# A hybrid attention and recurrence layer: the first block's keys beside the meta keys, squares by halves, and the last scalings shared with ScalarE

## The chip, the core and the metric

The kernel runs on one core of a Trainium2 chip. The metric is the device time of one execution in microseconds (us). PE is TensorE, the matmul engine; DVE is VectorE, ACT ScalarE, POOL GpSimd; SP is the engine whose queue issues most of the loads. "PEld" in a view is PE's loading of stationary operands.

## What is computed

One decoder layer over 1024 tokens of width 1024, with 16 learned meta tokens put ahead of them (1040 rows in all):

```
u = rmsnorm(h, g_pre_mix);  q, k, v, xr, yr = split(u @ w_in)
attn = sliding_window_attention_with_sinks(q, k, v, sinks)   # window 128
rec  = gelu(yr) * rg_lru(conv4(xr))                          # gated recurrence
h = h + rmsnorm(concat(attn, rec) @ w_out, g_post_mix)
u = rmsnorm(h, g_pre_ffn)
h = h + rmsnorm(square(relu(u @ w_ff1)) @ w_ff2, g_post_ffn) # d_ff = 4096
return h[16:]
```

Attention has 8 query heads of 64 and 2 key heads. Queries are taken in blocks of 128. A block sees the 128 keys before it and its own 128; for the first block of real tokens the keys before it are 112 places of padding, which are masked, and the 16 meta tokens. RMSNorm multiplies a row by (mean of squares + 1e-6) to the power -1/2.

## The kernel before, in words

Everything is in float32. A matmul of full precision is made of three: each operand is split into a high part, rounded to the format fp32r, and a low part, the rest; the product is high x high + high x low + low x high (`mm3`, lines 125 to 127; `part`, line 253, does one of the three at a time). The high part is cast on ACT (line 96 in `split`, 309 in `high_w`), the low part is a subtraction on DVE (lines 99 and 313).

The work has these stages in time.

1. **Rows and projections** (about 0 to 58 us). Rows of x come in eight blocks of 128, the meta rows ahead of the first. `norm_rows` (from line 222) squares a block on ACT with the row sum as by-product (line 225), forms rstd on POOL in two steps (lines 164 and 170: add eps, power -1/2) and scales the rows on DVE (line 231). PE transposes them against an identity (line 322); ACT and DVE evict high and low parts, times the norm's gain (lines 117 and 118). For the first 272 columns (meta rows and two blocks) the order on ACT and on DVE is written out by hand: `chained(0, ...)` strings ACT's instructions, `chained(1, ...)` DVE's. ACT's string is: high part of the key weights, the eight evictions, high part of the v weights, of the q weights, the squares of row blocks 3 and 4, the evictions of keys and v, the high part of the x weights. The squares of later row blocks are not in that string.
2. **The keys.** `sink_k` (lines 390 and 394) writes the keys' high and low parts, each head in its half of the partitions. The first projected piece holds 16 meta columns and 256 real ones. The meta keys go to `km`, a constant tile of four parts (head, high or low) of 128 columns, of which the last 16 hold keys and the rest zeros; the real ones go to `khh` (high) and `kl`. A DMA on POOL's queue copies the other half of the partitions (line 489).
3. **Attention** (about 58 to 187 us), in eight steps: four query pairs j times two halves of four blocks. `scores` makes, for each of two heads, a PSUM bank for two blocks at a time: q's block is the stationary operand, keys the moving one, 256 columns high (line 581) and 256 low (line 585). For block 0 that is done in four matmuls of 128 columns: the padded meta keys from `km`, then the first block from `khh` and `kl`. ACT copies scores (599), DVE picks between the two key blocks (600), takes the minimum (607), ACT the exponential (82), DVE scales (616); `attend` transposes on PE (630), splits, masks on POOL (635) and multiplies with v (646). Projections of later queries, of the recurrence's inputs and of its gates (`next_fill`) run between as filling work of lower priority.
4. **The recurrence**, the output projection and the first feed-forward product (to about 560 us).
5. **The second feed-forward product**, from there to the end, as seven products in place of eight (`PLAN`), each of eight steps. In the last product the last three steps are kept back and done output block by output block (`finish_late`), so that blocks 0, 1 and 2 can be finished while PE works on the next; block 3's columns are done in two pieces of 256. Finishing is: add the last product into the sum (`combine`, line 951), square it with the row sum (line 1284 on ACT, or line 1334 on DVE for block 3), root on ACT (line 82), reciprocal on DVE (189), scale by rstd and gain, and write. Blocks 0 to 2 are scaled by DVE in one instruction of 1024 columns (line 1327) and added into `out` by an accumulating DMA on POOL's queue (line 1331). For block 3 the multiplication by the gain is done ahead of the root (line 951) and two instructions scale and add the residual (line 1345). `finish_half` (line 1306) prepares the halves that are complete earlier.

Where no order is written out, a planner simulates the program with estimated costs and emits each engine's instructions in the order that comes out, by priority (place in the program) among what is ready. `behind(name, ins)` holds an instruction behind another in that order without a semaphore. On the chip each engine works through its list in order.

Tiles come from slots with tags: "ws" has 4, "b" 17, "c" 8, "d" 4, "e" 2, "raw" 2; a new tile of a tag waits until the oldest one's readers are done. PSUM has eight banks, two of each tag "acc", "s", "pt" and "o".

At the very start PE multiplies zeros (`load`, line 284), 7 times 512 and 6 times 256 columns; their result is not read. The zeros were those of `km`, cast by DVE (line 274) from a cleared tile.

## Time and profile before

| what | us |
|---|---|
| time before, median of 3 runs | 959.34 (959.26 to 960.56) |
| the profiled execution | 958.7 |
| its span, first to last instruction | 956.9 |
| PE busy in the span | 944.2 |
| DVE, ACT, POOL busy | 658.8, 501.9, 127.5 |

All views below come from that one profiled execution. Their times count from the start of the span. A timeline row gives start, duration, engine, line of the kernel, operation, tiles (written <- read), shape, and in brackets the idle time of the engine ahead of it with what ended that. The row of a matmul includes the filling of the array, so rows that follow each other on PE overlap; from start to start is what one costs. Where a row says x13, thirteen instructions are merged.

### The profile page before, as it was taken

How to read it: one execution, taken by the hardware profiler on the slowest of the kernel's cores; microseconds unless marked ns; L12 is line 12 of the kernel's file. 1: busy time of each engine (PE TensorE's matmuls, PEld its weight loads, DVE VectorE, ACT ScalarE, POOL GpSimd, SP SyncE). 2: the span in 40 equal slices, each digit the busy share in tenths (PEclk: the TensorE clock that was granted, in tenths of full speed). 3: DMA queues.
4: the chain of work that ended last, by engine and by line, in shares of the span. 5: the costliest groups of instructions: out<-in, count | busy, mean ns of one | idle time of the engine just before them, and what ended most of it. 6: DMA issues, size and time to landing. Idle time of an engine off the chain costs nothing.

```text
span 956.9 us, 12402 instructions
## 1 busy us (share of the span) xinstructions
PE 944.2 (99%) x4731; PEld 789.3 (82%) x4731; DVE 658.8 (69%) x841; ACT 501.9 (52%) x845; POOL 127.5 (13%) x186
## 2 busy tenths in 40 slices
PE   8999999999999999999999999999999999999996
PEld 7999999877888877888888888888888788888885
DVE  6567987879855776665644465476576776769884
ACT  7536666568645554434555575663533343445441
POOL 4102655410021100000000000001111100001201
PEclk9999999999999999999999999999999999999999
DMA  8221101104226466585532354324767765637934
GB/s 268 57 66 23 46 23 46 45 23 122 83 110 192 133 204 214 182 270 164 176 108 90 110 185 124 110 89 132 176 176 176 209 208 179 196 132 205 237 65 88
DMA packets 88183, 130.14 MB, mean 136 GB/s; under 512 B 13718, under 2 KB 52646, under 8 KB 88124
## 3 DMA queue, kind: packets, MB, share of 16 engines
q1 hardware_dynamic: 79532, 106.54, 34.0%
q0 software_dynamic: 8160, 21.51, 10.7%
q10 hardware_dynamic: 432, 1.31, 0.4%
q8 instruction: 37, 0.61, 0.3%
q14 instruction: 22, 0.18, 0.1%
HBM read 109.93 MB, written 18.87 MB: 135 GB/s over the span
## 4 chain that ended last, share of the span: by engine, by line
PE 94%; DVE 3%; ACT 1%; POOL 0%; DMA 0%; issue 0%; SPq 0%; DVEq 0%; POOLq 0%; ACTq 0%
PE ps_acc L125 11%; PE ps_acc L126 11%; PE ps_acc L127 11%; PE ps_pt L125 7%; PE ps_pt L126 6%; PE ps_pt L127 6%; PE ps_s L127 6%; PE ps_s L126 6%; PE ps_s L125 6%; PE ps_o L127 5%; PE ps_o L125 5%; PE ps_o L126 5%; PE ps_o L646 1%; PE ps_acc L253 1%; PE ps_o L925 1%; PE ps_s L581 1%
## 5 line engine op out<-in xcount | busy, mean ns | idle before, releaser
L96 ACT CAST ws<-raw 128x1024 fp32r<-128x1024 f32 (+1 forms) x68 | 69.6, 1024 | 117.8 <-PE ps_o L126 47.6
L99 DVE TENSOR_TENSOR ws<-raw,ws 128x1024 fp32r<-128x1024 f32 (+1 forms) x69 | 82.4, 1194 | 52.7 <-ACT ws L96 52.7
L125 PE MATMUL ps_acc<-a,ws 128*128 128x256 f32 (+2 forms) x256 | 86.1, 336 | 0.0
L126 PE MATMUL ps_acc<-a,ws 128*128 128x256 f32 (+2 forms) x256 | 85.4, 333 | 0.0
L127 PE MATMUL ps_acc<-a,ws 128*128 128x256 f32 (+2 forms) x256 | 85.0, 333 | 0.0
L99 DVE TENSOR_TENSOR b<-b,b 128x1024 fp32r<-128x1024 f32 (+2 forms) x50 | 58.9, 1178 | 26.5 <-PE ps_o L126 17.7
L96 ACT CAST ws<-e 128x1024 fp32r<-128x1024 f32 x41 | 42.9, 1047 | 64.3 <-PE ps_o L126 41.2
L96 ACT CAST b<-b 128x1024 fp32r<-128x1024 f32 (+2 forms) x49 | 50.0, 1020 | 43.8 <-DVE b L951 38.3
L99 DVE TENSOR_TENSOR ws<-e,ws 128x1024 fp32r<-128x1024 f32 x41 | 50.1, 1223 | 24.2 <-ACT ws L96 24.2
L635 POOL TENSOR_SCALAR_AFFINE_SELECT c<-c 128x512 fp32r<-128x512 f32 x64 | 53.7, 857 | 70.5 <-ACT c L96 60.7
L125 PEld LDWEIGHTS ps_acc<-a,ws 128*128 128x128 f32 x256 | 48.3, 189 | 4.8 <-issue 0.2
L126 PEld LDWEIGHTS ps_acc<-a,ws 128*128 128x128 f32 x256 | 48.2, 188 | 4.4 <-issue 0.4
L127 PEld LDWEIGHTS ps_acc<-a,ws 128*128 128x128 f32 x256 | 48.2, 188 | 4.4
L126 PE MATMUL ps_acc<-ws,b 128*128 128x512 f32 (+1 forms) x120 | 46.2, 385 | 0.6 <-DVE ws L99 0.6
L125 PE MATMUL ps_acc<-ws,b 128*128 128x512 f32 (+1 forms) x120 | 46.2, 386 | 0.0
L127 PE MATMUL ps_acc<-ws,b 128*128 128x512 f32 (+1 forms) x120 | 46.2, 385 | 0.0
L125 PE MATMUL ps_pt<-ws,b 128*128 128x512 f32 x112 | 44.4, 396 | 0.0
L126 PE MATMUL ps_pt<-ws,b 128*128 128x512 f32 x112 | 44.1, 394 | 0.0
L127 PE MATMUL ps_pt<-ws,b 128*128 128x512 f32 x112 | 44.0, 393 | 0.0
L125 PE MATMUL ps_s<-ws,b 128*128 128x512 f32 x110 | 43.4, 395 | 0.0
L127 PE MATMUL ps_s<-ws,b 128*128 128x512 f32 x110 | 43.3, 394 | 0.0
L126 PE MATMUL ps_s<-ws,b 128*128 128x512 f32 x110 | 43.3, 393 | 0.0
(399 smaller groups left out, 2658.7 us busy)
## 6 DMA issues: line engine op xcount, KB each, us to landing
raw<-in_w_ff_dram SPq DMA_DIRECT2D x61, 512.0 KB, 4.5
e<-in_w_ff_dram SPq DMA_DIRECT2D x45, 512.0 KB, 3.4
d<-in_w_ff_dram SPq DMA_DIRECT2D x12, 512.0 KB
s_dram<-d POOLq DMA_DIRECT2D x12, 512.0 KB, 4.1
raw<-in_w_in_dram SPq DMA_DIRECT2D x9, 512.0 KB
c<-in_x_dram SPq DMA_DIRECT2D x8, 512.0 KB
d<-in_x_dram SPq DMA_DIRECT2D x8, 512.0 KB, 3.2
out_dram<-raw SPq DMA_DIRECT2D x8, 512.0 KB
```

What stands on the lines that cost most here:

```text
L96: nc.scalar.copy(hi, src)
L99: low = nc.vector.tensor_tensor(lo, src, f32(hi), op=ALU.subtract).ins
L125: nc.tensor.matmul(dst, lh, rh, start=start, stop=False, skip_group_check=True)
L126: nc.tensor.matmul(dst, lh, rl, start=False, stop=False, skip_group_check=True)
L127: last_mm[0] = nc.tensor.matmul(dst, ll, rh, start=False, stop=stop, skip_group_check=True).ins.name
L253: last_mm[0] = nc.tensor.matmul(acc[:, :n], w[k // 2][:, kc, :], u[kc][k % 2][:, t0 : t0 + n], start=k == 0 and kc == 0, stop=k == last an ...
L581: nc.tensor.matmul(dst, q[h][:, c], hi, start=True, stop=False, skip_group_check=True,)
L635: nc.gpsimd.affine_select(out=p_[:, :, s], in_=f32(p_[:, :, 0]), pattern=[[0, 4], [g, P]], compare_op=op, fill=0.0, base=0, channel_multip ...
L646: nc.tensor.matmul(po[:, oc : oc + n], v, p_[:, pc : pc + n], start=first and k == 0, stop=last and k == 1, skip_group_check=True,)
L925: nc.tensor.transpose(pt[:, i, :], xn[:, kc * P : (kc + 1) * P], ident)
```

## The change

Four edits.

1. `km` becomes a tile of four parts of 256 columns: 112 zeros, 16 meta keys, and the 128 keys of the first block, which `sink_k` writes in the same instructions as the meta keys (64 x 144 in place of 64 x 16) and the DMA copies to the other half. They are written to `khh` and `kl` as well, as before. Block 0's scores then take two matmuls of 256 columns in place of four of 128. The tile is no longer a constant; it takes a slot of tag "e", the third one asked for, after the raw weights of q and of x; POOL clears it.
2. The zeros for the first products are a cleared "ws" tile, without the cast. All 13 zero products come first, and after each of the eight groups of transposes of the first 272 columns one more of 128 columns is put behind.
3. `norm_rows` of row blocks 1 and 2 (`fast`): ACT squares one half of the columns, DVE the other, POOL adds the two sums (eps is in DVE's) and takes the power, and DVE scales in two pieces of 512.
4. At the end, for blocks 0 to 2 the squares' by-product goes to PSUM. For block 2 the second half is multiplied by the gain beforehand (in `finish_half`), DVE scales only the first half and ACT the second. For block 3's first 256 columns ACT squares in place of DVE and adds the sum so far with one more small instruction; DVE's products by the gain are held behind its squares.

```diff
+        if fast:
+            ss = [small.tile([P, 1], F32, name=f"hq{i}", tag=f"hq{i}") for i in range(2)]
+            nc.scalar.activation(
+                xn[:, :512], src[:, :512], AF.Square, scale=RMS_SC, accum_out=ss[0]
+            )
+            nc.vector.tensor_tensor_reduce(
+                out=xn[:, 512:], in0=src[:, 512:], in1=src[:, 512:], scale=RMS_SC * RMS_SC,
+                scalar=EPS, op0=ALU.mult, op1=ALU.add, accum_out=ss[1],
+            )
+            rs = small.tile([P, 1], F32, name="rs", tag="rs")
+            nc.gpsimd.tensor_tensor(ss[0], ss[0], ss[1], op=ALU.add)
+            nc.gpsimd.tensor_tensor(rs, ss[0], half_pow, op=ALU.pow)
+            for i in range(2):
+                c = slice(512 * i, 512 * i + 512)
+                nc.vector.tensor_scalar(xn[:, c], src[:, c], rs, None, op0=ALU.mult)
+            return xn
...
-    zero = slot("ws", [P, 512])
-    nc.vector.memset(zero, 0.0)
-    km = const.tile([P, 4, P], F32R, name="km")
+    zeros = slot("ws", [P, 512], F32R)
+    nc.vector.memset(f32(zeros), 0.0)
-    nc.vector.tensor_copy(km.rearrange("p a b -> p (a b)"), zero)
...
-    cold = load(7, 512)
+    load(7, 512)
+    load(6, 256)
...
+            if b == 0:
+                load(1, P, ins.ins.name)
...
-    load(6, 256, cold)
...
     low_w(wq, rq)
+    km = slot("e", [P, 4, 2 * P], F32R)
+    nc.gpsimd.memset(f32(km[:, 0:2, 0 : P - NMETA]), 0.0)
+    nc.gpsimd.memset(f32(km[:, 2:4, :]), 0.0)
...
-            m, mk = slice(0, NMETA), slice(P - NMETA, P)
+            m, mk = slice(0, NMETA + P), slice(P - NMETA, 2 * P)
...
-                        qk(sp_[:, i, 0:P], b, km[:, h, :], km[:, 2 + h, :])
-                        qk(sp_[:, i, P:256], b, khh[h][:, 0:P], kl[h][:, 0:P])
+                        qk(sp_[:, i, :], b, km[:, h, :], km[:, 2 + h, :])
...
+        if j > 1:
             behind(w_low[0], combine(o[:, c], acc[:, c], gffn_b[:, c], ALU.mult))
...
             if j < 3:
+                rs = root_rstd(squares(y[k], acc[:, c], 0), ssq)
+                done_ = COLS[0] if j == 2 else slice(0, D)
                 w_low[0] = nc.vector.scalar_tensor_tensor(
-                    o, acc, root_rstd(squares(o[:, c], acc[:, c], 0), ssq), gffn_b,
+                    o[:, done_], acc[:, done_], rs, gffn_b[:, done_],
                     op0=ALU.mult, op1=ALU.mult,
                 ).ins.name
+                if j == 2:
+                    nc.scalar.activation(o[:, COLS[1]], o[:, COLS[1]], AF.Copy, scale=rs)
...
+            if k == 0:
+                part = squares(y[k], acc[:, c], 0)
+                nc.scalar.activation(part, part, AF.Identity, bias=ssq)
+            else:
+                part = small.tile([P, 1], F32, name="part", tag="part")
+                w_low[0] = nc.vector.tensor_tensor_reduce(
+                    out=o[:, c], in0=acc[:, c], in1=acc[:, c], scale=RMS_SC * RMS_SC,
+                    scalar=ssq, op0=ALU.mult, op1=ALU.add, accum_out=part,
+                ).ins.name
...
-            w_low[0] = combine(o[:, c], acc[:, c], gffn_b[:, c], ALU.mult).name
+            ins = combine(o[:, c], acc[:, c], gffn_b[:, c], ALU.mult)
+            if k == 1:
+                behind(w_low[0], ins)
+            w_low[0] = ins.name
```

More of the change, by code (lines that the diff above doesn't have):

```diff
@@ L220, in hybrid_layer, with norm_rows @@
     RMS_SC = 1.0 / math.sqrt(D)
-    def norm_rows(src, n, link=False):
+    def norm_rows(src, n, link=False, fast=False):
         xn = slot("d", [P, D])
+        if fast:
[14 more added lines that the diff above has]
+            return xn
         ssq = small.tile([P, 1], F32, name="ssq", tag="ssq")
@@ L268, in hybrid_layer @@
         nc.gpsimd.memset(f32(kl[h][HALF[1 - h]]), 0.0)
-    zero = slot("ws", [P, 512])
-    nc.vector.memset(zero, 0.0)
-    km = const.tile([P, 4, P], F32R, name="km")
+    zeros = slot("ws", [P, 512], F32R)
+    nc.vector.memset(f32(zeros), 0.0)
     vm = const.tile([P, 2, P], F32R, name="vm")
-    nc.vector.tensor_copy(km.rearrange("p a b -> p (a b)"), zero)
     flip = [0]
     idle = bank("acc")
-    zeros = km.rearrange("p a b -> p (a b)")
     def load(n, cols, after=None):
@@ L296, in normed @@
         rows += [(xt[2 * b], P), (xt[2 * b + 1], P)]
-        return [(norm_rows(s[:m], m), m) for s, m in rows]
+        return [(norm_rows(s[:m], m, fast=b == 0 and m == P), m) for s, m in rows]
     last = [None, None]
@@ L486, in hybrid_layer @@
     for h in range(2):
-        r, o, m = HALF[h], HALF[1 - h], slice(P - NMETA, P)
+        r, o, m = HALF[h], HALF[1 - h], slice(P - NMETA, 2 * P)
         nc.gpsimd.dma_start(f32(khh[h][o]), f32(khh[h][r]))
@@ L1326, in finish_late @@
             if j < 3:
+                rs = root_rstd(squares(y[k], acc[:, c], 0), ssq)
+                done_ = COLS[0] if j == 2 else slice(0, D)
                 w_low[0] = nc.vector.scalar_tensor_tensor(
-                    o, acc, root_rstd(squares(o[:, c], acc[:, c], 0), ssq), gffn_b,
+                    o[:, done_], acc[:, done_], rs, gffn_b[:, done_],
                     op0=ALU.mult, op1=ALU.mult,
                 ).ins.name
+                if j == 2:
+                    nc.scalar.activation(o[:, COLS[1]], o[:, COLS[1]], AF.Copy, scale=rs)
                 nc.gpsimd.dma_start(out[j * P : (j + 1) * P, :], o, accum_op=ALU.add)
                 continue
-            part = small.tile([P, 1], F32, name=f"part{k}", tag=f"part{k}")
-            nc.vector.tensor_tensor_reduce(
-                out=o[:, c], in0=acc[:, c], in1=acc[:, c], scale=RMS_SC * RMS_SC,
-                scalar=ssq, op0=ALU.mult, op1=ALU.add, accum_out=part,
-            )
+            if k == 0:
[7 more added lines that the diff above has]
+                ).ins.name
             ssq = part
```

## The prediction

> **What bounds the kernel now.** I read the page first: the span, the busy times and the chain that ended last; then the waits of PE, to see where it ever stood still.

> ```profile
> span 956.9 us, 12402 instructions
> PE 944.2 (99%) x4731; PEld 789.3 (82%) x4731; DVE 658.8 (69%) x841; ACT 501.9 (52%) x845; POOL 127.5 (13%) x186
> ...
> PE 94%; DVE 3%; ACT 1%; POOL 0%; DMA 0%; issue 0%; SPq 0%; DVEq 0%; POOLq 0%; ACTq 0%
> ```

> ```profile
> PE ps_acc L284 <- DVE km L274: 2.4, 1, 2.4
> PE ps_acc L125 <- ACT a L1136: 0.7, 1, 0.7
> PE ps_o L322 <- DVE d L231: 0.6, 2, 0.5
> PE ps_acc L126 <- DVE ws L99: 0.6, 1, 0.6
> PE ps_o L646 <- POOL c L635: 0.6, 1, 0.6
> ```

> PE is busy for 944.2 of 956.9 us and carries 94% of the chain. In between it waits 4.9 us in all, half of it before its first instruction; the other idle time is the tail after its last matmul. So microseconds come from three places only: matmul time itself, those waits, and the tail. A microsecond taken from another engine in the middle is worth nothing unless it ends one of the waits.

> The profiled execution took 958.7 us (1.8 us outside its span), 0.6 under the median of the three timed runs, 959.34. I make the sum against 958.7 and carry the difference over to the median.

> **The start.** Columns of the timeline: start, duration, engine, line, tiles, shape, and in brackets the idle time and what ended it.

> ```profile
> 1.09 2.11 POOL L268 MEMSET b<- 64x1024 f32 x2
> ...
> 1.49 0.83 DVE L274 CAST km<-ws 128x512 fp32r<-128x512 f32 x1
> ...
> 2.38 4.61 PE L284 MATMUL ps_acc<-km 128*128 128x512 f32 x13 [2.38 <-DVE km L274]
> ...
> 6.33 1.06 ACT L225 ACTIVATE d<-c 128x1024 f32<-128x1024 f32 x1 [0.51 <-DMA c<-in_x_dram]
> ...
> 8.47 0.75 DVE L231 TENSOR_SCALAR d<-c,rs 128x1024 f32<-128x1024 f32 x1 [0.81 <-POOL rs L170]
> 8.49 1.05 ACT L309 CAST b<-raw 128x1024 fp32r<-128x1024 f32 x1 [1.02 <-DMA raw<-in_w_in_dram]
> ...
> 9.64 0.49 ACT L117 ACTIVATE a<-ps_o,gcol 128x272 fp32r<-128x272 f32 x1
> ...
> 12.83 4.19 PEld L253 LDWEIGHTS ps_acc<-a,b 128*128 128x128 f32 x33 [0.19 <-ACT a L117]
> ...
> 15.71 1.22 DVE L313 TENSOR_TENSOR ws<-e,ws 128x1024 fp32r<-128x1024 f32 x1
> ...
> 18.36 1.06 ACT L225 ACTIVATE d<-c 128x1024 f32<-128x1024 f32 x1 [1.61 <-DMA c<-in_x_dram]
> ...
> 19.41 0.73 ACT L390 CAST b<-ps_acc 64x256 fp32r<-64x256 f32 x2
> 20.16 0.36 ACT L390 CAST km<-ps_acc 64x16 fp32r<-64x16 f32 x2
> ...
> 20.82 1.05 ACT L309 CAST ws<-e 128x1024 fp32r<-128x1024 f32 x1
> ...
> 21.92 2.04 PEld L253 LDWEIGHTS ps_acc<-a,ws 128*128 128x128 f32 x16
> ```

> **Zeros.** The 0.83 us cast of km goes and PE can multiply zeros at about 1.5 instead of 2.38. Those products are thrown away (the six narrower ones already ran ahead, all 13 are in one row), so the 0.9 us less in the first wait is worth nothing by itself. The eight new 128-wide zero products sit where PE is paced by ACT (it still waits for ACT before 12.83): cost 0, and 8 x 0.11 = 0.9 us (the narrow matmul's time, worked out below) if that cover were gone.

> **Squares by halves.** Now the second row block's square takes ACT 1.06 us from 6.33, then POOL, then DVE's scaling until 9.22. Half a row on ACT (0.63 for 128x512, row at the end) saves about 0.4. DVE's half is not in the trace in this form: 256 columns take it 0.48 (L1334, below), so 512 lie between 0.48 and 0.96; I take 0.75, since 256 and 512 columns of an addition take 0.41 and 0.69. POOL's two steps stay two. The scaling in two pieces costs one more fixed part, about 0.1. If DVE has the second block's square queued behind both scalings of the first, 0.85 us, the 0.4 is gone and xn comes some 0.3 late.

> None of it reaches the end. ACT's first eviction (9.64) has to follow the cast of the key weights, which starts at 8.49 when their DMA lands and ends at 9.54: 0.1 us to be had, whatever the squares do. And there is a second gate. ACT's queue holds the square of the fifth row block ahead of the key eviction; that square waits for its DMA until 18.36. From there ACT runs without a pause: square, keys 19.41, meta keys 20.16, v, cast of the x weights 20.82 to 21.87; PE starts on these weights at 21.92. PE arriving 0.1 earlier or 0.3 later at 21.9 finds nearly the same gate. I take 0, bounds 0.2 gained and 0.3 lost.

> **The wider meta tile costs at that gate.** The two casts of 64x16 (0.18 each) become 64x144. Between 64x16 and 64x256 (0.365 each) a column costs 0.8 ns, so 128 more are 0.1 each: **0.2 us lost**, since everything up to the cast of the x weights moves. Bounds: 0, if the planner puts the keys ahead of that square; 0.4 at the price of 64x256. DVE's two subtractions grow alike; behind them waits the low part of the x weights, which PE asks for only after 16 products with the high part, 2.04 us from 21.92. The wider copies by DMA are wanted at 58.7 (row below).

> km now lies in a slot of tag "e", so POOL may clear it only when the q weights in that slot are split (15.71 + 1.22 = 16.93). POOL's clearing: 1.05 us per 1024 columns, 224 + 512 columns, 0.76 us, done at 17.7 if the queue is free; ACT writes km at 20.16. Behind the clearing stand POOL's rstd steps of the next rows, which PE transposes just before 21.92. All hidden, with 2.4 us of slack; beyond that ACT's queue stops at km, with v and the x weights behind it and PE behind these, and each us costs one. The slot's next user is the gates' weights after the last score (153), so no load waits.

> **Scores.** This is the term that counts.

> ```profile
> L581 PE MATMUL ps_s<-km,b x8: 221/222/307, 58.7 to 153.4; 128*128 128x128 f32 x8
> ```

> ```profile
> 73.04 0.22 PE L581 MATMUL ps_s<-km,b 128*128 128x128 f32 x1
> ...
> 74.20 0.39 PE L126 MATMUL ps_acc<-a,ws 128*128 128x512 f32 x1
> ...
> 79.22 0.28 PE L581 MATMUL ps_s<-b,b 128*128 128x256 f32 x1
> ...
> 80.17 0.60 PE L630 MATMUL ps_pt<-ident,c 128*128 128x128 f32 x4
> ```

> A group with the first block is ten matmuls, four of them 128 wide: 74.20 - 73.04 = 1.16 us. A group without it is eight of 256: 80.17 - 79.22 = 0.95, or 0.119 each. So the four narrow ones cost 1.16 - 6 x 0.119 = 0.45, 0.11 each: hardly less than wide ones. Two wide ones in their place save 0.21, in eight groups 1.7 us.

> [...]

> Does PE time count there?

> ```profile
> 20.00:185.00 165.00, 164.91 (x1222) 155.84 (x1220) 128.19 (x242) 99.99 (x294) 63.93 (x94) 1.00 0.17 44
> ```

> ```profile
> 100.00:120.00 20.00, 20.00 (x135) 18.27 (x134) 19.49 (x31) 13.26 (x40) 10.68 (x16) 1.00 0.19 54
> ...
> 900.00:930.00 30.00, 30.00 (x156) 25.49 (x155) 29.53 (x31) 15.53 (x24) 2.42 (x2) 1.00 0.51 123
> ```

> ```profile
> 151.08 0.77 ACT ws L96
> ...
> 185.50 1.25 PE ps_o L646 x9
> ```

> (Windows: length, then busy time of PE, PEld, DVE, ACT, POOL.) The chain stays on PE up to 151, where ACT takes it over from the scores, and comes back at 185.50 after 0.6 us of waiting. Between, PE works but is not what ends last. Seven of the eight groups lie before 151, the last at 153. I count seven: **1.5 us gained**; bounds 0, if other engines hold the stage, and 1.7.

> **The end.**

> ```profile
> 936.85 0.69 DVE L951 TENSOR_TENSOR a<-ps_acc,a 128x512 f32<-128x512 f32 x1 [6.93 <-PE ps_acc L127]
> ...
> 945.69 0.63 ACT L1284 ACTIVATE a<-a 128x512 f32<-128x512 f32 x1 [3.12 <-DVE a L951]
> ...
> 947.44 1.28 DVE L1327 SCALAR_TENSOR_TENSOR a<-a,rs,a 128x1024 f32<-128x1024 f32 x1
> ...
> 948.63 0.48 DVE L1334 CUSTOM_DVE_ANT_0 a<-a,late 128x256 f32<-128x256 f32 x1
> ...
> 948.90 0.28 PE L127 MATMUL ps_acc<-a,b 128*128 128x256 f32 x1
> ...
> 949.15 0.42 DVE L951 TENSOR_TENSOR a<-a,a 128x256 f32<-128x256 f32 x1
> 949.50 0.41 DVE L951 TENSOR_TENSOR a<-ps_acc,a 128x256 f32<-128x256 f32 x1
> ```

> PE's last matmul ends at 949.18, but DVE adds its result only at 949.50, being busy with block 2's scaling (1.28), the square of block 3's first quarter (0.48) and its product (0.42). After: half the scaling, 0.69, to 948.1; the product to 948.5; DVE waits for PE at 949.18. The last addition comes **0.3 us earlier** and with it all that follows. ACT has three instructions more of at most 0.63 each after 947.4: through by 949.3, and its sum is asked for at 949.6. Squares written to PSUM in place of SBUF I count alike; the block's output goes out earlier, which nothing waits for. Bounds 0 and 0.4. The multiplication brought forward (0.69 on DVE, which is 29.53 of 30 busy up to 930) stands behind the split of a later step's weights; the 6.93 us that DVE idles before 936.85 cover it; else it costs 0.7.

> **Sum.** -1.5 - 0.3 + 0.2 = -1.6 us: 957.1 against 958.7, and 957.7 against the median. That is 0.17%, under the 0.2% (1.9 us) that a measurement of this kernel can tell from no change.

> **Rivals.**

> *PE's time is not passed on.* DVE is at 19.49 of 20 us from 100 to 120, and POOL ended a PE wait at 185.5. If the attention chain keeps its pace, PE only waits longer. Then -0.3 + 0.2: **959.2**. Against it: PE's row has 164.91 of 165 us busy up to the wait at 185, and ACT and DVE are released by the scores. [...]

> *The order falls out well.* The order on each engine is planned anew. If the keys get ahead of the waiting square, the 0.2 is not lost and the 0.2 of the start is kept; if the wait at 185.5 closes, 0.6 more: 957.7 - 1.0 = **956.7**. For it: both waits are products of one order. Against: nothing in the change asks for it.

> *PE stays at half speed*, on the slow side.

> ```profile
> L284 PE MATMUL ps_acc<-km x13: 388/628/792, 2.4 to 6.6; 128*128 128x512 f32 x7, 128*128 128x256 f32 x6
> ```

> A 512-wide zero product takes 628 ns, later ones 390: the zeros warm PE up. With them from 1.5 on they end about 0.9 us earlier, with little behind them until the rows come. Should PE fall back, the 33 matmuls from 12.83 (4.19 us, 0.127 each) take twice that; past 1.6 us lost, 13 of them, the change is slower; all 33 give +2.6: **961.9**. Against: the eight zero products are put there. [...]

> **How the numbers follow.** Forecast 50%, its own range 957.1 to 958.9; not passed on 18%; good order 22%; half speed 10%. Faster by over 0.2% (under 957.4): a third of the forecast and nearly all of the good order, 0.39. Slower (over 961.3): most of the last case, 0.07. The rest, 0.54. The range, 956.0 to 960.0, takes in the first three cases with the bounds of their terms (-1.7, -0.4, -0.2 and the closed wait's 0.6 below; no merge gain and 0.4 + 0.3 lost at the start above) and some tenths of scatter, and leaves out half speed.

> **What would show it.** Right: the score groups with km take 0.95; PE's wait at 185.5 grows slightly; the last DVE addition follows PE's last matmul at once; PE starts on the x weights some 0.2 later than 21.92. Wrong: a new wait of PE between 20 and 185, zeros' successors at 0.25 each, or ACT waiting for POOL before km.

## The result and the profile after

| | kernel before | changed kernel |
|---|---|---|
| median, us (22 executions of each) | 961.25 (959.26 to 963.86) | 959.10 (957.11 to 962.38) |
| the profiled execution | 958.7 | 961.16 |
| its span | 956.9 | 959.5 |
| ratio after / before | | 0.9975, interval 0.9967 to 0.9984 |

The change makes the kernel faster by 0.25%, some 2.4 us (0.16 to 0.33%; 2.15 us between the medians). Forecast were 1.6 us, and 957.7 us as the time; 959.1 lies in the range, but 1.4 us over the forecast although the gain was larger: the base had been taken as 959.34, the median of three executions, and over 22 it is 961.25. Moreover, the profiled execution of the changed kernel is 2.5 us *longer* than that of before. One profile of each can't be compared by its length here; both have to be taken apart by place. The changed kernel's page first:

```profile
span 959.5 us, 12392 instructions
PE 947.1 (99%) x4723; PEld 792.0 (83%) x4723; DVE 658.9 (69%) x845; ACT 501.6 (52%) x849; POOL 126.8 (13%) x188
...
PE 88%; DVE 5%; DMA 2%; ACT 2%; POOL 1%; issue 1%; DVEq 0%; SPq 0%; ACTq 0%; POOLq 0%
```

PE is busy for 2.9 us more than before (944.2), though it has eight products fewer: a busy PE need not be a fast one. And 2% of the chain are DMA, which had none. Next PE's waits (engine, line, releaser: us in all, times, longest):

```profile
PE ps_acc L297 <- DVE base_e L537: 1.5, 1, 1.5
PE ps_s L127 <- DVE e L99: 0.7, 1, 0.7
PE ps_o L336 <- DVE d L239: 0.7, 1, 0.7
PE ps_acc L125 <- ACT a L1154: 0.7, 1, 0.7
PE ps_s L336 <- DVE d L248: 0.5, 1, 0.5
PE ps_o L664 <- POOL c L653: 0.3, 1, 0.3
```

Against before: the wait at the end of attention (L646, now L664) fell from 0.6 to 0.3, where the forecast had it grow; the wait of `ps_s L127` for DVE is new. Its place is 365 us. Four places make up nearly all of the 2.5 us: 3.6 - 2.1 + 1.4 - 0.3.

**Attention.** The start of the last transposes of v and of the first gate matmul, in the timelines of before and of after:

```profile
64.74 0.38 PE L554 MATMUL ps_pt<-ident,c 128*128 128x128 f32 x2
...
197.78 0.43 PE L772 MATMUL ps_s<-b,e 64*128 64x348 f32 x1
```

```profile
68.29 0.38 PE L573 MATMUL ps_pt<-ident,c 128*128 128x128 f32 x2
76.61 0.28 PE L600 MATMUL ps_s<-e,b 128*128 128x256 f32 x1
...
77.54 0.39 PE L127 MATMUL ps_acc<-a,ws 128*128 128x512 f32 x1
...
199.26 0.43 PE L790 MATMUL ps_s<-b,e 64*128 64x348 f32 x1
```

133.04 us before, 130.97 after: **2.07 us gained**. A group of scores with the meta keys takes 77.54 - 76.61 = 0.93, where the prediction had named 0.95 as the sign of being right.

**The start.** It gave 3.6 us away in this execution:

```profile
8.49 1.05 ACT L323 CAST b<-raw 128x1024 fp32r<-128x1024 f32 x1 [1.42 <-DMA raw<-in_w_in_dram]
...
14.60 6.04 PEld L270 LDWEIGHTS ps_acc<-a,b 128*128 128x128 f32 x37
...
20.89 0.75 ACT L408 CAST b<-ps_acc 64x256 fp32r<-64x256 f32 x2 [1.59 <-PE ps_acc L270]
21.66 0.57 ACT L408 CAST e<-ps_acc 64x144 fp32r<-64x144 f32 x2
...
22.26 1.06 ACT L242 ACTIVATE d<-c 128x1024 f32<-128x1024 f32 x1
...
23.72 1.05 ACT L323 CAST ws<-e 128x1024 fp32r<-128x1024 f32 x1
...
25.50 1.55 PEld L270 LDWEIGHTS ps_acc<-a,ws 128*128 128x128 f32 x12
```

The key matmuls take 6.04 us for 37, 0.163 each in the mean, where before had 0.127 (4.19 for 33): from start to start 0.23 until 17.6 us and 0.13 after. PE runs at half clock until then: the trace's records of the granted clock begin at 17.6 us here and at 6.8 before (the windows' clock column counts from there only and shows 1.00 for the stretch ahead; the weight loads' durations tell the truth, 330 ns until 17.1 us and 188 from 17.8 on). The half is read where a record covers such a stretch: 0.50 in this kernel's second profile, below. So ACT waits for PE's keys (1.59 us ahead of 20.89), and PE starts on the x weights at 25.5 in place of 21.92. The keys are cast ahead of the fifth row block's square (22.26), as the rival "the order falls out well" had it, but the half clock had made that square's turn late as well.

**Loads at 353 to 368 us.** DVE's wait for one load, before and after:

```profile
359.15 0.69 DVE L951 TENSOR_TENSOR a<-raw,a 128x512 f32<-128x512 f32 x1 [4.85 <-DMA raw<-in_w_ff_dram]
```

```profile
362.13 0.69 DVE L969 TENSOR_TENSOR a<-raw,a 128x512 f32<-128x512 f32 x1 [6.29 <-DMA raw<-in_w_ff_dram]
```

1.44 us longer, and PE has to wait at 365 us. The semaphore events show why: each of these loads lands in 16 parts. Before, all 16 came between 358.86 and 359.06; after, 15 came by 360.52 and the last at 362.04.

**The end.** The last rows on DVE, before and after:

```profile
949.50 0.41 DVE L951 TENSOR_TENSOR a<-ps_acc,a 128x256 f32<-128x256 f32 x1
949.95 0.48 DVE L1334 CUSTOM_DVE_ANT_0 a<-a,part 128x256 f32<-128x256 f32 x1
...
951.01 1.42 DVE L1345 SCALAR_TENSOR_TENSOR a<-a,rs,d 128x512 f32<-128x512 f32 x2
```

```profile
952.01 0.42 DVE L969 TENSOR_TENSOR a<-ps_acc,a 128x256 f32<-128x256 f32 x1 [0.69 <-PE ps_acc L127]
952.59 0.48 DVE L1361 CUSTOM_DVE_ANT_0 a<-a,sq 128x256 f32<-128x256 f32 x1
...
953.65 1.42 DVE L1375 SCALAR_TENSOR_TENSOR a<-a,rs,d 128x512 f32<-128x512 f32 x2
```

Now DVE waits for PE (0.69) and adds 0.31 us after the last matmul's start (951.70), where it took 0.60 before (948.90): the forecast 0.3. But the square follows 0.58 after the addition in place of 0.45: DVE's stream has a semaphore instruction for ACT's sum there, at 952.48, though that sum was done at 951.22. So the last scaling starts 1.95 after that matmul in place of 2.11: 0.16 remain. The writing behind it is shorter too, by 0.1 to 0.5 us in the profiles of kernels with this end, so 0.3 (here) to 0.7 us are gained in all.

### The profile page after: what moved, and what is told of

Read it like the earlier page. It is cut to its first block, busy times and chain, and to the rows that moved or that the text cites. A ratio compares the mean times of both kernels' runs of the same rounds, so it can differ in the third digit from the quotient of the medians.

```text
span 959.5 us, 12392 instructions
## 1 busy us (share of the span) xinstructions
PE 947.1 (99%) x4723; PEld 792.0 (83%) x4723; DVE 658.9 (69%) x845; ACT 501.6 (52%) x849; POOL 126.8 (13%) x188
## 4 chain that ended last, share of the span: by engine, by line
PE 88%; DVE 5%; DMA 2%; ACT 2%; POOL 1%; issue 1%; DVEq 0%; SPq 0%; ACTq 0%; POOLq 0%
PE ps_acc L126 10%; PE ps_acc L125 10%; PE ps_acc L127 10%; PE ps_pt L125 6%; PE ps_pt L127 6%; PE ps_pt L126 6%; PE ps_s L127 6%; PE ps_s L126 6%; PE ps_s L125 6%; PE ps_o L127 5%; PE ps_o L126 5%; PE ps_o L125 5%; PE ps_acc L270 1%; PE ps_o L664 1%; POOL c L653 1%
## 5 line engine op out<-in xcount | busy, mean ns | idle before, releaser
L96 ACT CAST ws<-raw 128x1024 fp32r<-128x1024 f32 (+1 forms) x68 | 69.7, 1024 | 124.4 <-PE ps_o L126 46.4
L99 DVE TENSOR_TENSOR ws<-raw,ws 128x1024 fp32r<-128x1024 f32 (+1 forms) x69 | 82.3, 1193 | 46.7 <-ACT ws L96 45.7
L125 PE MATMUL ps_acc<-a,ws 128*128 128x256 f32 (+2 forms) x256 | 85.8, 335 | 0.0
L127 PE MATMUL ps_acc<-a,ws 128*128 128x256 f32 (+2 forms) x256 | 85.2, 333 | 0.0
L126 PE MATMUL ps_acc<-a,ws 128*128 128x256 f32 (+2 forms) x256 | 85.1, 333 | 0.0
L99 DVE TENSOR_TENSOR b<-b,b 128x1024 fp32r<-128x1024 f32 (+2 forms) x50 | 58.9, 1178 | 27.8 <-PE ps_o L126 18.7
L96 ACT CAST ws<-e 128x1024 fp32r<-128x1024 f32 x41 | 42.9, 1047 | 65.4 <-PE ps_o L126 48.8
L96 ACT CAST b<-b 128x1024 fp32r<-128x1024 f32 (+2 forms) x49 | 50.0, 1020 | 44.7 <-DVE b L969 39.2
L99 DVE TENSOR_TENSOR ws<-e,ws 128x1024 fp32r<-128x1024 f32 x41 | 50.1, 1222 | 18.6 <-ACT ws L96 18.5
L125 PEld LDWEIGHTS ps_acc<-a,ws 128*128 128x128 f32 x256 | 48.3, 189 | 4.6 <-issue 0.2
L127 PEld LDWEIGHTS ps_acc<-a,ws 128*128 128x128 f32 x256 | 48.2, 188 | 4.5
L126 PEld LDWEIGHTS ps_acc<-a,ws 128*128 128x128 f32 x256 | 48.2, 188 | 4.4 <-issue 0.4
L126 PE MATMUL ps_acc<-ws,b 128*128 128x512 f32 (+1 forms) x120 | 46.3, 386 | 0.2 <-DVE ws L99 0.2
L125 PE MATMUL ps_acc<-ws,b 128*128 128x512 f32 (+1 forms) x120 | 46.2, 386 | 0.0
L127 PE MATMUL ps_acc<-ws,b 128*128 128x512 f32 (+1 forms) x120 | 46.2, 385 | 0.0
L125 PE MATMUL ps_pt<-ws,b 128*128 128x512 f32 x112 | 44.3, 396 | 0.0
L126 PE MATMUL ps_pt<-ws,b 128*128 128x512 f32 x112 | 44.1, 394 | 0.0
L127 PE MATMUL ps_pt<-ws,b 128*128 128x512 f32 x112 | 44.1, 393 | 0.0
L125 PE MATMUL ps_s<-ws,b 128*128 128x512 f32 x110 | 43.4, 395 | 0.0
L127 PE MATMUL ps_s<-ws,b 128*128 128x512 f32 x110 | 43.3, 394 | 0.0
L126 PE MATMUL ps_s<-ws,b 128*128 128x512 f32 x110 | 43.3, 393 | 0.0
```

The costliest lines, as they stand in the source:

```text
L96: nc.scalar.copy(hi, src)
L99: low = nc.vector.tensor_tensor(lo, src, f32(hi), op=ALU.subtract).ins
L125: nc.tensor.matmul(dst, lh, rh, start=start, stop=False, skip_group_check=True)
L126: nc.tensor.matmul(dst, lh, rl, start=False, stop=False, skip_group_check=True)
L127: last_mm[0] = nc.tensor.matmul(dst, ll, rh, start=False, stop=stop, skip_group_check=True).ins.name
```

## The experiments

Each place is read off as a stretch between two starts of PE's instructions, so that a kernel late at the start isn't late everywhere. The table collects the profiles, in us. "Clock" is where the records of the granted clock rise (a fall between two rises is marked). "x weights" is PE's first matmul on them. "Attention" is the stretch above, against before's. "Late part" is by how much the last of 16 parts of a load came after the 15 others, in the loads around 357 us and around 740 us (the largest one; a dash where none was late by 0.6 or more).

| kernel | clock up at | x weights | attention | late part, 357 | late part, 740 |
|---|---|---|---|---|---|
| before | 6.8 | 21.93 | 0 | - | 1.4 |
| changed | 17.6 | 25.53 | -2.07 | 1.6 | - |
| changed, again | 5.0, fall 8.4, 11.8 | 23.25 | -2.08 | 1.3 | - |
| keys alone | 6.9 | 22.10 | -2.08 | 1.3 | 0.7 |
| front alone | 5.5, fall 9.0, 12.4 | 22.95 | 0 | - | - |
| end alone | 11.6 | 22.52 | 0 | - | 0.9 |
| long zeros | 7.0 | 22.17 | -2.08 | 1.1 | - |
| long zeros, count restored | 4.7 | 22.23 | -2.06 | - | 1.1 |
| the same, squares undone | 4.9 | 22.85 | -2.07 | - | 1.4 |
| the same, none interleaved | 5.2 | 22.23 | -2.08 | - | 1.5 |
| changed, count restored | 6.5, fall 9.9, 16.8 | 24.81 | -2.06 | - | 0.9 |
| squares alone | 5.8, fall 9.2, 16.0 | 23.92 | 0 | - | 1.6 |
| no zeros | 12.3 | 22.62 | 0 | 0.8 | - |
| before, long zeros | 6.8 | 22.09 | 0 | - | 1.3 |

**The three parts, one at a time.** First the keys: `km` widened as in the change, the zeros left to a constant tile of the old size.

```diff
+    km = slot("e", [P, 4, 2 * P], F32R)
...
-                        qk(sp_[:, i, 0:P], b, km[:, h, :], km[:, 2 + h, :])
-                        qk(sp_[:, i, P:256], b, khh[h][:, 0:P], kl[h][:, 0:P])
+                        qk(sp_[:, i, :], b, km[:, h, :], km[:, 2 + h, :])
```

> The kernel before with the wider meta tile alone (block 0's scores in two wide matmuls; the zeros, squares and the end as before). Theory: this edit carries most of the change. Between the v transposes (64.9) and the gates (201.4) the two profiles shown are 2.05 us closer in the changed kernel, so the time falls by 1.5 to 2.1 us, ratio 0.998 to 0.9985. Rival, that the gain comes from the earlier zeros: ratio 0.9995 to 1.0005 here.

Measured: 959.07 us, ratio 0.9981 (0.9971 to 0.9992). The whole of attention's gain is there (-2.08). At the start, with the clock up at 6.9, the order of before stands, and the wider casts are read off directly:

```profile
20.12 0.57 ACT L393 CAST e<-ps_acc 64x144 fp32r<-64x144 f32 x2
...
21.00 1.05 ACT L309 CAST ws<-e 128x1024 fp32r<-128x1024 f32 x1
...
22.02 0.85 DVE L397 TENSOR_TENSOR b<-ps_acc,b 64x256 fp32r<-64x256 f32 x2
22.88 0.62 DVE L397 TENSOR_TENSOR e<-ps_acc,e 64x144 fp32r<-64x144 f32 x2
23.54 1.23 DVE L313 TENSOR_TENSOR ws<-e,ws 128x1024 fp32r<-128x1024 f32 x1
```

0.57 in place of 0.36, the cast of the x weights at 21.00 in place of 20.82, PE on them at 22.10: the 0.2 that was forecast. The planner's order here also puts DVE's scaling of a further row block ahead of the keys' low parts (22.02, 20.55 before), so that the x weights' low part is done at 24.77 and PE waits for it: 0.9 us lost, about 0.5 of it at that wait and the rest just behind it, in this kernel alone. The forecast's cover ("PE asks for it only after 16 products") holds by some tenths only.

Second the front: the new zeros and the squares by halves.

```diff
+    zeros = slot("ws", [P, 512], F32R)
+    load(7, 512)
+    load(6, 256)
...
+            if b == 0:
+                load(1, P, ins.ins.name)
...
+        return [(norm_rows(s[:m], m, fast=b == 0 and m == P), m) for s, m in rows]
```

> The kernel before with the zeros' and the squares' edits alone (meta tile and end as before). Theory: nothing in the median, ratio 0.9995 to 1.0005, because PE's start on the x weights is set by the wait of ACT, or, where the clock rises late, by the clock. Rival, that earlier zeros raise the clock earlier in most executions: 1 to 2 us less, ratio 0.998 to 0.999. Second rival, that less zero work behind the zeros' end lets the clock rise later than before on average: 1 us more, ratio 1.001.

Measured: 960.11, ratio 0.9995 (0.9982 to 1.0008): nothing. Third the end alone, `finish_half` and the finishing functions of the change in the kernel before:

```diff
+                rs = root_rstd(squares(y[k], acc[:, c], 0), ssq)
+                done_ = COLS[0] if j == 2 else slice(0, D)
...
+            if k == 0:
+                part = squares(y[k], acc[:, c], 0)
```

> The kernel before with the shared last scalings alone. Theory: the last DVE addition follows PE's last matmul at once; 0.3 us less from PE's last matmul to the end of the span, ratio 0.9997, inside the scatter of the times, so it is read from the profile: 7.7 us from PE's last end to the span's end fall to 7.4. Rival, that the multiplication brought forward delays the last steps: PE shows a new wait after 920.

Measured: 959.98, ratio 0.9997 (0.9984 to 1.001), too small for the times; in its profile the stretch from the last matmul to the end is 0.6 us shorter. The three ratios multiply to 0.9973, the change's 0.9975: the parts add up as far as intervals of 0.0010 to 0.0013 on each can tell, and the keys, the only part whose interval leaves out 1, carry the gain.

**Long zeros: is the scatter the clock's?** The changed kernel with unbroken zeros at the start, to see whether the 4 to 5 us between executions go with the moment of the clock's rise (6.8 us in the profile of before, 17.6 in the changed kernel's).

```diff
-    load(7, 512)
-    load(6, 256)
+    load(16, 512)
```

> The changed kernel with sixteen zero products of 512 columns at the start in place of seven of 512 and six of 256: twice 3.4 us at half speed, from 1.5 to 8.3. [...] Then the clock is up by 8.4 in every execution, the times lie within 1.5 us of each other and the median falls by 1.5 to 2.5 us against the changed kernel: ratio to before 0.9955 to 0.996. Rival, that the scatter comes from elsewhere (loads' landing): the scatter stays and the ratio is 0.9975 as with the change.

Measured: 957.24, ratio 0.9971 (0.996 to 0.9982), 955.33 to 959.44. A miss in part: only 0.0004 of ratio under the change's, and the scatter of 4 us stays. The clock rose at 7.0 and PE was on the x weights at 22.17, so the start was repaired. None of the 12 executions had a mean granted clock of 0.996 or less, and still they lie 4.1 us apart: the scatter is not the clock's alone.

**The change once more**, for a second profile (no edit).

> The changed kernel once more, for a second profile of it. Theory 'the clock's rise is an accident of the execution': the granted clock may rise at another moment than 17.6 us, and the start of the x weights follows it: 22.1 to 22.4 us if it rises by 8, 25 or later if it rises after 16. Rival 'the new zero products hold the clock down': it rises at 16 to 18 us again and the x weights start at 25.5 again. Both: the stretch from the last transposition of the values to the gates is again about 2.1 us shorter than before's, and the wait for the loads of raw from in_w_ff_dram at 353 to 368 us is again about 1.5 us longer than before's, because the instruction count at that place is the same. Time against the kernel before: ratio 0.996 to 0.999.

Measured: 958.75, ratio 0.9981 (0.997 to 0.9992). The same program now rose at 5.0, fell at 8.4, rose at 11.8; here and in the kernel below with "none interleaved", windows of the start (length, busy time of PE, PEld, DVE, ACT, POOL, then the granted clock):

```profile
5.00:8.40 3.40, 1.40 (x13) 1.10 (x12) 2.49 (x7) 1.11 (x4) 3.24 (x5) 1.00 0.98 300
8.50:11.70 3.20, 3.20 (x19) 2.81 (x17) 1.90 (x7) 2.44 (x5) 0.11 (x1) 0.50 1.30 251
```

```profile
5.00:8.40 3.40, 2.93 (x26) 2.70 (x26) 2.50 (x7) 1.10 (x4) 3.24 (x5) 1.00 1.03 309
8.50:11.70 3.20, 3.08 (x19) 2.02 (x18) 2.51 (x8) 3.08 (x7) 0.04 (x1) 1.00 1.28 248
```

In the changed kernel PE is busy for 1.40 of 3.40 us, then gets 0.50 of the clock for the next stretch; in the other it is busy for 2.93 and keeps 1.00. The late loads at 357 us came again (6.08 us of DVE's wait), so they belong to the program; the moments of the clock don't.

**The instruction count.** The page of the profile lists a DMA queue of the kind "instruction", q8, with 37 packets and 0.61 MB, so 16 KB each; one takes 0.9 to 1.8 us. That they carry PE's instructions is my estimate: 37 of them make 64 bytes for each of the 9462 matmuls and weight loads of the kernel before. The change drops 16 matmuls and their 16 weight loads ahead of 350 us, of which the eight new zero products bring half back, and the next such packet comes later. In the changed kernel it falls into the burst of loads (352 to 365 us; queue, kind: packets, MB, share):

```profile
q8 instruction: 1, 0.02, 0.5%
```

Before has no such row there: its packet starts at 350.2, ahead of the burst, after's at 357.7. In all 14 profiles the packet's place sorts the kernels here: five have a late part, and their packet started 1.3 to 2.1 us ahead of the late load's first part; in the other nine it started 4.7 us or more ahead of the burst's first load. The test adds nothing but products, the columns of zeros at the start being the same 8192:

```diff
-    load(16, 512)
+    load(11, 512)
+    load(10, 256)
```

> The kernel of the long zeros with 11 products of 512 columns and 10 of 256 in place of 16 of 512: the same 8192 columns, but five more products, ten more instructions in TensorE's stream, which brings the stream's count back to that of the kernel before at every place after the key scores. Theory 'an instruction fetch of 16 KB falls into the burst of the loads and makes one DMA engine late': the fetch comes at 349 to 350.5 us again, ahead of the burst, all 16 parts of the loads land within 0.3 us, and the stretch 353 to 368 takes what it takes before (the kernel of the long zeros loses 0.5 us there, the change 1.45). Time 0.3 to 0.6 us under the long zeros where their clocks rise alike. Rival 'the late DMA engine comes from something else that the keys' edit moves': the stretch stays 0.5 us or more above before's.

Measured: 957.07, ratio 0.9961 (0.9948 to 0.9974). The packet came at 348.5, DVE waited 4.9 us, the stretch takes what it took before: as the theory had it. The same test on the changed kernel itself, 5120 columns cut finer:

```diff
-    load(7, 512)
-    load(6, 256)
+    load(4, 512)
+    load(7, 256)
+    load(10, P)
```

> The changed kernel with its 5120 columns of zeros at the start cut into 4 products of 512, 7 of 256 and 10 of 128 columns in place of 7 and 6: eight products, 16 instructions more in TensorE's stream, and nothing else. At 350 us the stream then stands where the kernel before's stands. Theory 'the changed kernel's late loads come from the instruction fetch in their midst': the fetch at 349 to 352 us, the DVE's wait for raw from in_w_ff_dram 4.8 to 5.0 us in place of 6.1 to 6.3, the stretch 353 to 368 as before's; 1.2 to 1.4 us shorter than the changed kernel where their clocks rise alike, ratio to the kernel before 0.9955 to 0.9975. Rival 'the late part comes from the keys' edit in another way': the wait stays at 6 us or more and the time that of the changed kernel.

DVE's wait there in the timeline; then PE in the windows 350 to 372 and 736 to 756 us, and the same two windows of the changed kernel:

```profile
359.93 0.69 DVE L970 TENSOR_TENSOR a<-raw,a 128x512 f32<-128x512 f32 x1 [4.81 <-DMA raw<-in_w_ff_dram]
```

```profile
350.00:372.00 22.00, 22.00 (x93) 17.06 (x94) 14.70 (x23) 10.61 (x17) 2.16 (x4) 1.00 0.66 214
...
736.00:756.00 20.00, 19.27 (x84) 15.33 (x83) 13.09 (x13) 7.16 (x7) 2.42 (x2) 1.00 0.71 182
```

```profile
350.00:372.00 22.00, 20.34 (x84) 15.24 (x84) 14.37 (x23) 10.58 (x17) 1.94 (x4) 1.00 0.58 191
...
736.00:756.00 20.00, 20.00 (x88) 16.25 (x87) 14.68 (x14) 7.37 (x7) 3.62 (x3) 1.00 0.85 205
```

The wait is as the theory had it: 4.81 for 6.29, and PE without a gap. The time misses: 959.65, ratio 0.9989 (0.9976 to 1.0001), no better than the change. For the profiled execution (959.17) two reasons stand in the rows. The clock fell at 9.9 again (x weights at 24.81). And the restored count brought back a late part at 740 us: PE is busy for 19.27 of 20 us there, the change for all 20. The kernel before has that loss as well:

```profile
736.00:756.00 20.00, 19.38 (x84) 15.41 (x83) 13.98 (x13) 8.30 (x8) 2.42 (x2) 1.00 0.70 188
```

So the shifted count costs the change 1.2 to 1.4 us at 357. At 740 it goes with 0.4 to 0.9 us less (from 720 to 748 us, in the change's two profiles against before's), but that the packet is the cause there is not shown. Of the 14 profiles, the eight of kernels whose count at that place is before's, or six instructions above it, have a late part of 0.9 or more, the six others 0.7 or none; yet the packet's place does not sort them. In the changed kernel a packet from 740.9 to 741.8 lies in a load that lands from 741.1 to 742.0 with no part late; in "before, long zeros" the packet was over at 736.0, and the load that came late began to land at 739.4.

**The squares.** The halves alone in the kernel before:

```diff
+        return [(norm_rows(s[:m], m, fast=b == 0 and m == P), m) for s, m in rows]
```

> The kernel before with the squares of the first two row blocks by halves on ScalarE and VectorE alone, its zero products as before. Theory 'the squares were not what the start waits for': the second block's normalised rows are ready 0.0 to 0.3 us later than before's 9.22 us, GpSimd's power takes 1 us or more beside VectorE where it took 0.57, and the x weights start at 21.9 to 22.2 us where the clock rises by 8; time 0.0 to +0.3 us. Rival 'the squares gain and the zeros lose': the x weights start 0.2 us or more before 21.9, and the time is 0.2 us or more shorter.

Measured: 960.54, ratio 0.9995 (0.9984 to 1.0006): no difference in the time. The power, expected at 1 us or more, took 0.55 for the first block there; it began ahead of DVE's second square. And the other way, the halves undone in the kernel with the restored count (`fast=False`):

> The kernel e6_fetch_back with the squares undone (each row's square whole on one engine, as before): keys, end, long zeros, count of instructions restored. Theory 'the squares gain nothing': the same time as e6_fetch_back within 0.3 us, the transpositions of the second block start at 9.2 to 9.4 us. Rival 'the squares gain': 0.2 us or more longer. Against the kernel before, if keys (-2.1), end (-0.3 to -0.5) and the restored fetch (0) add up and the clock rises by 8 us: 2.2 to 2.6 us shorter, ratio 0.9970 to 0.9980.

Measured: 957.53, ratio 0.9969 (0.9955 to 0.9982), 0.46 us over its base, less than the intervals tell, though the theory had 0.3 at most and the rival 0.2 or more. In its profile the second block's transposes start at 9.79 (forecast 9.2 to 9.4) in place of 9.17, and PE is on the x weights 0.62 later. First its base, then this kernel:

```profile
6.08 0.63 ACT L227 ACTIVATE d<-c 128x512 f32<-128x512 f32 x1 [0.64 <-DMA c<-in_x_dram]
...
9.17 0.33 PE L336 MATMUL ps_o<-ident,d 128*128 128x128 f32 x1
```

```profile
6.67 1.06 ACT L242 ACTIVATE d<-c 128x1024 f32<-128x1024 f32 x1 [0.22 <-DMA c<-in_x_dram]
...
9.79 0.33 PE L336 MATMUL ps_o<-ident,d 128*128 128x128 f32 x1 [0.76 <-DVE d L248]
```

The second block's rows landed 0.59 later there, and in the 14 profiles that moment lies anywhere from 5.9 to 6.7 us, with the halves or without, so this pair tells little of them. Over all 14 the second block's first transpose starts at 8.8 to 9.4 us in the eight with the halves and at 9.2 to 9.8 in the six without: they do bring PE some 0.3 us, as its first half is scaled sooner. Where ACT's cast of the x weights is the gate that is worth nothing, as the prediction had it. In the kernel above the cast was done at 22.11 and PE came only at 22.85; there a gain of some tenths is possible, and the intervals leave it open. The changed kernel's timeline shows why the halves bring no more:

```profile
4.67 0.69 DVE L230 CUSTOM_DVE_ANT_0 d<-c 128x512 f32<-128x512 f32 x1 [3.20 <-DMA c<-in_x_dram]
...
6.04 1.55 POOL L236 TENSOR_TENSOR rs<-hq,half_pow 128x1 f32<-128x1 f32 x1
...
7.63 0.88 DVE L239 TENSOR_SCALAR d<-c,rs 128x512 f32<-128x512 f32 x2 [0.44 <-POOL rs L236]
```

DVE's half took 0.69 (0.75 forecast), but POOL's power for the first block took 1.55 beside DVE's work, where it takes 0.57 in the kernel before, and DVE waited for it. From the start of the second block's square to its scaled rows 3.11 us pass in the changed kernel (6.35 to 9.46), 2.89 before (6.33 to 9.22), and 2.82 in "squares alone", where the power was not stretched (6.49 to 9.31).

**No zeros at all** (the kernel before without its 13 products, which compute nothing that is used):

```diff
-    cold = load(7, 512)
...
-    load(6, 256, cold)
```

> The kernel before without its 13 zero products, which compute nothing that is used. Theory 'the start is priced by the moment at which TensorE's clock rises': the rise comes at 11 us or later, as work on TensorE begins only at 6.8 us; for each us that it rises after 7 the x weights start 0.25 to 0.35 us later (3.6 us for 17.6 against 6.8 in the profiles so far, 2.0 for 16.0 after a fall at 9.2), so 23.5 to 26 us in place of 21.93, and the time is 1.5 to 4 us longer than a kernel before whose clock rose at 7. Against the kernel before's median, in which late rises are already mixed: 0.5 to 2.5 us longer. Rival 'the products of zeros do nothing for the clock': the rise at 6 to 8 us, x weights at 21.9 to 22.2, time within 0.3 us.

Measured: 959.78 (959.23 to 960.77), ratio 0.9994 (0.9984 to 1.0004). Both theories miss. The clock rises at 12.3, without a fall, and PE is on the x weights at 22.62, only 0.7 late: half a clock until 12.3 us mostly hides behind ACT's gate at 22 us; until 16.0 to 17.6 it costs 2.0 to 3.6. The 13 products gain nothing that the interval can tell, and the scatter is 1.5 us without them and 3.9 with them: in four profiles with such products the clock fell again, at 8.4 to 9.9 us, and it did not in the one without.

**None interleaved**: the kernel with long zeros and restored count, without the eight products among the transposes.

```diff
-    load(11, 512)
-    load(10, 256)
+    load(3, 512)
+    load(26, 256)
...
-            if b == 0:
-                load(1, P, ins.ins.name)
```

> The kernel e6_fetch_back without the 8 products of zeros among the first transpositions; 3 products of 512 and 26 of 256 at the start instead, which keeps the columns at the start (8192) and the number of instructions. Theory 'the zeros among the transpositions only cost': the x weights start at 21.9 to 22.1 us (22.2 in e6_fetch_back) with the clock up at 5 us, the stretch 353 to 368 as in e6_fetch_back, time 0.1 to 0.3 us shorter than e6_fetch_back's. Rival 'they hold the clock up between the transpositions': the clock falls back after 8 us, as in e2_front_alone, e5_change_again and e7_squares_alone, the x weights start at 23 us or later and the time is 0.5 us or more longer.

Measured: 956.79 (956.41 to 957.86), ratio 0.9962 (0.9947 to 0.9977). The clock rose at 5.2 and held; the x weights began at 22.23, as with them. Here ACT's cast, done at 22.18, is the gate; with the eight products the cast was done at 21.97 and PE's own transposes lasted until then. That the start is the same is thus in part chance, but the clock did hold without them, and five executions show no loss. This one and "long zeros, count restored" (0.9961) are the fastest of the study, some 1.7 us under the changed kernel measured beside the latter (958.75).

**The base for the parts**: the kernel before with 16 unbroken products.

```diff
+    zeros = slot("ws", [P, 512], F32R)
-    cold = load(7, 512)
+    load(16, 512)
...
-    load(6, 256, cold)
```

> The kernel before with 16 unbroken products of zeros of 512 columns, from a tile of zeros of their own, in place of 7 of 512 and 6 of 256; its keys, squares and end as before. It is the base for the parts of the change: the same clock and the same place of the instruction fetch as in e6_fetch_back, e8_no_squares and e10_no_interleaved. Theory 'the parts add up to what the places in the trace show (keys -2.1, end -0.3 to -0.5, start +0.2)': the clock rises at 5 to 7 us and never falls back, the fetch lies ahead of the loads, and the time is 2.1 to 2.5 us over e10_no_interleaved's, 958.9 to 959.3 us; against the kernel before 0.5 to 1.5 us shorter (ratio 0.9985 to 0.9995), which is what the clock's falls cost it. Rival 'the change gains about 1 us more than its places show, elsewhere': the time is 3 us or more over e10_no_interleaved's, 959.8 us or more, and no shorter than the kernel before.

Measured: 958.83, ratio 0.9991 (0.9982 to 1.0). The rival's 959.8 is not reached. Against "none interleaved", with clock and fetch alike, the keys and the end are worth 958.83 - 956.79 = 2.0 us by the medians. But in the two comparisons the kernel before took 959.50 and 960.42; by the ratios it is 0.9991 - 0.9962 = 0.29%, 2.8 us, and the intervals allow some 1.7 us either way. The places say 2.1 + 0.3 to 0.7 - 0.2. So the parts agree with the places, and the rival's 1 us more, gained elsewhere, is not ruled out.

## Why the prediction was right, and where not

- **Scores, -1.5: right in kind, too small.** The stage gave 2.07, in eight profiles with the keys' edit alike. Eight groups of 0.21 are 1.7, not seven of them 1.5, and the wait for POOL at 185.5 closed by 0.3 in place of growing: 2.0 of the 2.07. The step that failed is "I count seven": ACT's taking over the chain at 151 did not cut off the last group. That PE's time is not passed on, is refuted here. The merged group takes 0.93 us for 1.16.
- **The end, -0.3: right in sum.** The addition comes 0.29 earlier; half of that is lost again before the square, and shorter writing makes up for it.
- **The wider casts, +0.2: right** in "keys alone", where the casts can be read off by themselves: PE is on the x weights 0.17 us later.
- **Squares and zeros, 0: right as far as the intervals tell**, with ACT's gate as the reason. How little the halves brought has a reason that the text did not have: POOL's power took 1.55 us beside DVE's work.
- **PE at half speed, 10%: it happened**, in the very execution that was profiled (+3.6 us at the start; that it was this one is luck). In the second profile it came as told, a rise at 5.0 and a fall at 8.4 behind zeros that had ended; in the first the clock had not risen at all before 17.6. The sign named for it, "zeros' successors at 0.25 each", is there (0.23). Its price was looked for in the 33 matmuls alone, but 1.8 of the 3.6 us were lost ahead of them (14.60 for 12.83). (The 628 ns named there is the median over both widths; the 512-wide products alone take 651 in the mean.) What was wrong is the comparison: the kernel before has it as well. Of its 98 executions measured beside the experiments, 24 had a mean granted clock of 0.996 or less, and in each set these took 1.6 to 2.3 us longer at the median than the rest; of the 45 with the change's own zeros (the change twice, front alone) it was 22, of the 43 of the four kernels with the long products of zeros and of the base, none. This mean shows falls only: the execution whose clock rose at 17.6 has 0.998. So half speed widens the scatter of both kernels, and no run shows that it decides their ratio.
- **Not foreseen: the instruction fetch**, +1.2 to 1.4 us at 357, and what goes with the count at 740, -0.4 to -0.9. The sum of places, -2.07 - 0.3 to 0.7 + 0.2 + 1.3 - 0.4 to 0.9, is -1.3 to -2.2 us, beside the measured -1.8 (second comparison) and -2.4 (0.16 to 0.33%). That the forecast's 1.6 came near is in part luck: the scores' extra 0.6 and this unforeseen loss nearly cancel.

The class forecast likeliest, within 0.2%, is missed by little: the gain is 0.25%, with 0.16% still in the interval, and 0.19% in the second comparison. What stays open: single places between 450 and 760 us still differ by 0.2 to 1.3 us between executions of like kernels. "End alone" has a late part at 740 us as well and lost nothing there, and "no zeros" lost time there with no part late. And no kernel moved the fetch alone out of both bursts.

## What to carry to other kernels

Two matmuls of 128 columns with fresh weights cost here nearly what two of 256 do (0.11 us each and 0.119), so merging them paid where PE was the chain, the last group of the stage included. Where a kernel is so close to its bound that 1 us counts, read the profile by stretches between landmarks: its length alone mixed 3.6 us of clock into a 2 us gain. With products of zeros that ran on, without a gap, until the real ones came, no execution here had the low mean clock of a fall (none of 43, against 22 of 45 with the change's own zeros); what that gained in time in the kernel before (0.09%, interval 0 to 0.18%) is hardly clear of the noise, and leaving them out cost nothing that the interval can tell.
